# Cache pages on GpSimd's queue, a later sum of log f, later first pages and gathered conv outputs in a recurrent-and-attention decoder step

## Chip, cores and metric

One core of one Trainium2 chip (trn2). The metric is the device time of one execution of the program in microseconds, of which the median over several runs is given. Below, PE is TensorE, DVE is VectorE, ACT is ScalarE, POOL is GpSimd and SP is SyncE, whose instruction stream is used here only to issue DMAs.

## What is computed

One layer of a decoder trunk on 512 prompt positions and 8 sample positions (520 columns), all with the same weights, in float32 with D = 1024. Cut to what matters:

```
h = RMSNorm(x) * (1 + scale1) + shift1                 # adaLN: scale, shift, gate from c @ ada_w
z = h @ w_in -> xr | gr | q | k | v | forget logits | gA | gB
branch A: xc = causal width-4 conv(xr); RG-LRU scan(xc); * gelu(gr); @ w_proj_a
          conv_new = last 3 inputs of the conv, per prompt and sample      (an output)
branch B: logf = log_sigmoid(fl + b_f)
          prompt: softmax(q k / 8 + sum of logf from key to query) v
          sample: the same, with 1024 past rows of each sample taken from pages of a cache
                  (8 samples x 8 pages of 128 rows; a page table says which)
x += gate1 * ((sigmoid(gA) * A @ w_proj_a + sigmoid(gB) * B @ w_proj_b) @ w_o)
x += gate2 * SwiGLU(RMSNorm(x) ...); final RMSNorm
```

The forget logits of prompt and samples give log f, which is an output too, and whose running sum over the prompt positions enters the scores.

## The kernel before

Everything lies transposed, features on the partitions and the 520 positions along the columns, in two halves of 260. A weight matrix is cut into units of 1024 x 128. SP loads two units at a time into a buffer `wraw` (there are two), ACT rounds a unit into a high part `whi`, DVE subtracts for the low part `wlo`, and PE makes each product of 128 output features from three matmuls (high x high, low x high, high x low) for each of the 8 slices of 128 rows and each half, 48 matmuls in all. `product` does this; its first step, `begin`, counts the product (`state["n"]`), calls `tick`, and then loads and splits weights ahead.

The order of the program's text is: q0 to q5 (by a code of their own), q6, q7 (products 0 and 1), then the recurrent stage in pairs of feature tiles (i = 0, 2, 4, 6): `conv(i)`, gates and gelu of the pair before, `conv(i + 1)`, `gate_a`, `lru_gates`, `gate_b`, `lru_exp`. These are products 2 (xr0) to 31 (gr7). Product 32 is k0, and then come the products with w_proj_a (pa0 to pa7) and v0, then attention, merge, w_o and the feed-forward part. The scheduler of the language may move an instruction within its engine, mostly close to its place in the text; each engine then runs its list in that order and waits where an operand or a buffer is not there.

Work on the cache is spread over the products by `tick`. `KEYS[n]` says how many key pages (or half-width pairs of pages, for the first two samples, while only one half of q is there) product n loads; `VALUES` are the products at which a page of values may be used. A page goes into one of seven buffers `pgp`, which the adaLN weights `araw` also use, by `page_load`: SP reads the page's number from the page table into a register (L617) and issues the load (L618); every fourth load back must have been issued first. `key_sums` does the dot products of loaded pages on DVE, a multiplication by the broadcast q (`qb`) and a reduction per head (L662, L663 for half-width pairs, L667, L668 for pages), `state["age"]` ticks after their load: 1 up to q7, 2 from xr0 on. For four pages (`POOL_KEYS`) the multiplication is POOL's (L649). `past_turn` and `past_sums` make the suffix sums of the past log f that `past_softmax` adds to the sums; `past_sums` is PE work (L398, L399).

`forget_logits` and `log_forget` make log f of the new positions. The logits go through DRAM to be spread over 128 partitions; a chain of some 20 small DVE instructions makes log f; it is stored as an output and to `lfd` in DRAM (L586, L587), read back with heads on partitions (L588), summed along the prompt by a DVE scan into `fcs` (L590), and that is stored (L591) for the attention stage.

`conv(i)` evacuates the product twice on ACT (L884, L885), adds the three delayed inputs on DVE (L893, L894), and has three POOL copies put the new conv state into `conv_out` (L895 to L897), which SP stores at the end of the stage (L1027).

Of the kernel before, what the change touches and what calls it, by code (L numbers as in the profile page):

```python
# [8 lines left out]
F32 = mybir.dt.float32  # L9
# [3 lines left out]
ALU = mybir.AluOpType  # L13
# [5 lines left out]
NP = 512  # L19
# [5 lines left out]
KT = 8  # L25
# [39 lines left out]
def kernel(ctx, tc, xT, par, gates, b_f, cst, cse, own, cache_k, cache_v, cache_lf, pt,  # L65
# [103 lines left out]
    def flush():  # L169
        while stores:  # L170
# [1 line left out]

    later = {}

    KEYS = dict(zip(range(42), (2, 0, 0, 2, 3, 2, 3, 2, 0, 1, 1, 1, 2, 2, 2, 1, 0, 1, 0, 1, 2, 2, 2, 2, 0, 1, 1, 1, 2, 2, 1, 2,
                                1, 1, 1, 1, 1, 1, 1, 1, 0, 0)))
# [400 lines left out]
    def log_forget():  # L577
        a = small("fa", 128, LC, 1)
        e = small("fe", 128, LC, 1)
        l1 = small("fl1", 128, LC, 1)  # L580
        sp.dma_start(a, flat(fld))
        act.activation(e, a, AF.Abs)
        act.activation(e, e, AF.Exp, scale=-1.0)
        log1p("fz", e, LC, l1)
        dve.scalar_tensor_tensor(a, a, 0.0, l1, ALU.min, ALU.subtract)
        sp.dma_start(flat(lfT), a)  # L586
        sp.dma_start(flat(lfd), a)  # L587
        sp.dma_start(lf, lfd)  # L588
        fcs = slot("fcs", NP, parts=H)
        dve.tensor_tensor_scan(fcs, one_col[:H].to_broadcast([H, NP]), lf[:, :NP], 0.0, ALU.mult, ALU.add)  # L590
        sp.dma_start(ftd, fcs)  # L591
# [15 lines left out]


    S = []
    loads = []  # L610

    def page_load(cache, s, j, pg=None, c0=0, c1=D):
        if pg is None:
            pg = pgp.tile([128, D], F32, name="pg", tag="pg")
        n = s * NPAGE + j
        with tc.issue_after(loads[-4].ins) if len(loads) >= 4 else nullcontext():
            r = sp.value_load(ptb[0:1, n:n + 1], min_val=0, max_val=NPOOL - 1)  # L617
        loads.append(sp.dma_start(pg, cache[bass.ds(r, 1), :, c0:c1].rearrange("a p c -> (a p) c")))  # L618
        return pg

    qb = {}
# [17 lines left out]
    def key_page(s, j, half=None):  # L639
        if half is not None:  # L640
            return key_halves(s, j, half)
        if j == 0:
            t = pgp.tile([128, D], F32, name="qb", tag="pg")
            sp.dma_start(t, qtd[s:s + 1, :].partition_broadcast(128))
            qb[0] = t
        pg = page_load(cache_k, s, j)
        late = s * NPAGE + j in POOL_KEYS
        if late:
            pool.tensor_tensor(pg, pg, qb[0], ALU.mult)  # L649
        pend.append([0, s, j, pg, None if late else qb[0], None])  # L650

    def key_sums():
        for p in pend:
            p[0] += 1
        while pend and pend[0][0] >= state["age"]:
            _, s, j, pg, q, half = pend.pop(0)
            r = s // 2
            c = 256 * (r % 2) + 32 * j + H * (s % 2)
            with tc.issue_after(state["last"].ins):
                if half is not None:  # L660
                    b, c = 8 * (r % 2) + j, H * (s % 2) + 8 * half
                    dve.tensor_tensor(pg, pg, q.unsqueeze(1).to_broadcast([128, 2, 512]), ALU.mult)  # L662
                    dve.tensor_reduce(S[r // 2].rearrange("p (b c) -> p b c", c=32)[:, b:b + 2, c:c + 8],  # L663
                                      pg.rearrange("p j (h d) -> p j h d", d=DH), AX.X, ALU.add)
                else:
                    if q is not None:
                        dve.tensor_tensor(pg, pg, q, ALU.mult)  # L667
                    dve.tensor_reduce(S[r // 2][:, c:c + H], pg.rearrange("p (h d) -> p h d", d=DH), AX.X, ALU.add)  # L668
# [159 lines left out]
    for i in range(KT):  # L828
# [45 lines left out]
    conv_out = keep.tile([128, KT, 27], F32, name="conv_out")  # L874
    rg_out = keep.tile([128, KT, 9], F32, name="rg_out")
    g = [None] * KT
    lru = {}

    def conv(i):
        xr, xc = slot("xr"), slot("xc")  # L880

        def evac(j, b):
            t0, t1 = HALVES[j]
            act.copy(xr[:, t0:t1], b)  # L884
            act.activation(xc[:, t0:t1], b, AF.Identity, scale=cw[3], bias=prm[:, i, P_CB:P_CB + 1])  # L885

        cw = [prm[:, i, P_CW + n:P_CW + n + 1] for n in range(4)]
        sc = prm[:, i, P_SC:P_SC + 24].rearrange("p (s n) -> p n s", n=3)
        co = conv_out[:, i, 3:27].rearrange("p (s n) -> p n s", n=3)
        product(f"xr{i}", h, evac)  # L890
        for n in range(3):
            d = 3 - n
            dve.scalar_tensor_tensor(xc[:, d:NP], xr[:, :NP - d], cw[n], xc[:, d:NP], ALU.mult, ALU.add)  # L893
# [65 lines left out]
    def both(fn, i):  # L959
        fn(i)  # L960
        fn(i + 1)
# [19 lines left out]
    state["age"] = 2  # L981
    for i in range(0, KT, 2):
        conv(i)
        if i == 0:
            q_done(*q_last)
            past_sums(0)
            ada_piece(1, 6)
            ada_load(1, 7)
        else:
            both(lru_root, i - 2)  # L990
            gelu(i - 2)
            lru_scan(i - 2)
        conv(i + 1)
        if i == 0:
            past_sums(1)
            ada_piece(1, 7)
            ada_copy(1)
        else:
# [4 lines left out]
        if i < 6:  # L1003
# [4 lines left out]
            gate_a(i + 1)  # L1008
            lru_gates(i + 1)
            gate_b(i)  # L1010
            gate_b(i + 1)
            both(lru_exp, i)
            if i == 2:
                log_forget()
        else:
            lru_gates(i)
            gate_a(i)
# [6 lines left out]
            both(lru_scan, i)  # L1024
            both(lru_mul, i)
            both(lru_g, i)
    sp.dma_start(convT, conv_out)  # L1027
    sp.dma_start(rgT, rg_out)

# [548 lines left out]
```

## Time and profile before

| | us |
|---|---|
| runs | 1097.44, 1098.28, 1098.85 |
| median | 1098.28 |
| the profiled execution | 1096.58 |
| its span, from first to last instruction | 1094.8 |
| PE busy | 1038.4 (95%) |
| DVE busy | 667.5 (61%) |
| ACT busy | 499.8 (46%) |
| POOL busy | 165.5 (15%) |

All views below are of the profiled execution, times in us from its first instruction. The chain that ended last is followed back from the last instruction, at each step to what released it; 71% of the span on it are PE's and 12% DVE's. In lists of waits the numbers are the total, how many times, and the longest. In rows of a stage stand its length and then the busy time of each engine with the number of its instructions, the clock granted to PE, the busy share of the DMA engines and GB/s. A row of the order of work has the start, the time taken, the engine (SPq is SP's sequencer), the source line and the operands, and in brackets how long the engine stood idle before it and what ended that. "L210" is a line of the kernel before.

### The profile page before, as it was taken

Reading aid. Unit: us, or ns where it says so; the run is one execution under the profiler, and the core shown is the slowest. Engines: PE = TensorE matmul, PEld = TensorE weight load, DVE = VectorE, ACT = ScalarE, POOL = GpSimd, SP = SyncE. Lnnn points to the kernel's source line nnn. Section 1 sums busy time; section 2 is a strip of 40 time slices with the busy share of each in tenths; the row PEclk is TensorE's granted clock in tenths of the full one; section 3 lists DMA queues with packets and bytes.
Section 4 is the critical chain, followed back from the end, with each engine's and each line's share of the span. In section 5 each row is a group of like instructions: output and inputs, shape, how many; then the busy total and the mean of one; then the engine's idle time right before and its main releaser. Section 6 shows DMA issues by size and latency. Waiting matters only on the chain.

```text
span 1094.8 us, 21019 instructions
## 1 busy us (share of the span) xinstructions
PE 1038.4 (95%) x8210; PEld 955.2 (87%) x8210; DVE 667.5 (61%) x1158; ACT 499.8 (46%) x972; POOL 165.5 (15%) x269
## 2 busy tenths in 40 slices
PE   4998999979999999989999999999999999999996
PEld 2876799969888987778888889999999999999995
DVE  5438699978979876667665544943343333433354
ACT  4513466746683256557787323542222223222352
POOL 1212100000403034325330001500000000000013
PEclk8999999999999999889999999999999999999998
DMA  9797985859777988889775683222232332323212
GB/s 331 261 305 268 325 299 161 267 161 304 243 231 250 320 263 260 248 249 255 231 235 175 232 298 108 79 78 78 90 104 78 103 90 78 116 78 95 79 59 79
DMA packets 167333, 206.95 MB, mean 189 GB/s; under 512 B 9778, under 2 KB 126018, under 8 KB 167170
## 3 DMA queue, kind: packets, MB, share of 16 engines
q1 hardware_dynamic: 163154, 197.62, 57.2%
q10 hardware_dynamic: 3680, 6.42, 1.6%
q0 software_dynamic: 400, 1.57, 0.5%
q8 instruction: 64, 1.05, 0.4%
q14 instruction: 35, 0.29, 0.1%
HBM read 192.49 MB, written 13.09 MB: 188 GB/s over the span
## 4 chain that ended last, share of the span: by engine, by line
PE 71%; DVE 12%; DMA 6%; ACT 5%; issue 3%; SPq 1%; POOL 1%; POOLq 0%; ACTq 0%; DVEq 0%
PE fig L245 11%; PE fiu L245 10%; PE fo L245 10%; PE pa L245 4%; PE pb L245 4%; PE v L245 3%; PE gb L245 3%; PE xr L245 3%; PE k L245 3%; PE wo L245 3%; PE pv L750 2%; DMA araw<-in_ada_w_dram 2%; PE qp L467 2%; DVE wlo L211 2%; DVE pg L667 2%
## 5 line engine op out<-in xcount | busy, mean ns | idle before, releaser
L211 DVE TENSOR_TENSOR wlo<-wraw,whi 128x1024 fp32r<-128x1024 f32 (+1 forms) x131 | 160.4, 1225 | 152.0 <-ACT whi L210 147.2
L210 ACT CAST whi<-wraw 128x1024 fp32r<-128x1024 f32 (+1 forms) x131 | 136.8, 1044 | 234.9 <-PE fo L245 74.5
L245 PE MATMUL fiu<-h2h,wlo 128*128 128x260 f32 x320 | 90.6, 283 | 0.0
L245 PE MATMUL fig<-h2h,wlo 128*128 128x260 f32 x320 | 90.5, 283 | 0.0
L245 PE MATMUL fig<-h2h,whi 128*128 128x260 f32 x320 | 90.3, 282 | 0.0
L245 PE MATMUL fiu<-h2h,whi 128*128 128x260 f32 x320 | 90.3, 282 | 0.0
L245 PE MATMUL fig<-h2l,whi 128*128 128x260 f32 x320 | 90.1, 282 | 0.0
L245 PE MATMUL fiu<-h2l,whi 128*128 128x260 f32 x320 | 90.1, 281 | 0.0
L245 PE MATMUL fo<-ach,wlo 128*128 128x260 f32 x292 | 82.6, 283 | 0.0
L245 PE MATMUL fo<-ach,whi 128*128 128x260 f32 x292 | 82.5, 283 | 0.0
L245 PE MATMUL fo<-acl,whi 128*128 128x260 f32 x292 | 82.4, 282 | 0.0
L337 POOL TENSOR_TENSOR ss<-ss,sq 128x260 f32<-128x260 f32 x18 | 13.6, 756 | 419.8 <-ACT sq L336 419.4
L245 PEld LDWEIGHTS fiu<-h2l,whi 128*128 128x128 f32 x320 | 60.5, 189 | 0.0
L245 PEld LDWEIGHTS fig<-h2l,whi 128*128 128x128 f32 x320 | 60.5, 189 | 0.0
L245 PEld LDWEIGHTS fiu<-h2h,whi 128*128 128x128 f32 x320 | 60.2, 188 | 0.0
L245 PEld LDWEIGHTS fig<-h2h,whi 128*128 128x128 f32 x320 | 60.2, 188 | 0.0
L245 PEld LDWEIGHTS fig<-h2h,wlo 128*128 128x128 f32 x320 | 60.2, 188 | 0.0
L245 PEld LDWEIGHTS fiu<-h2h,wlo 128*128 128x128 f32 x320 | 60.1, 188 | 0.0
L667 DVE TENSOR_TENSOR pg<-pg,qb 128x1024 f32<-128x1024 f32 x44 | 55.5, 1274 | 5.1 <-DMA pg<-in_cache_k_dram 5.0
L668 DVE TENSOR_REDUCE S<-pg 128x16 f32<-128x1024 f32 x48 | 57.5, 1207 | 0.2
L245 PEld LDWEIGHTS fo<-ach,whi 128*128 128x128 f32 x292 | 55.0, 188 | 0.0
L245 PEld LDWEIGHTS fo<-acl,whi 128*128 128x128 f32 x292 | 54.9, 188 | 0.0
(386 smaller groups left out, 3429.8 us busy)
## 6 DMA issues: line engine op xcount, KB each, us to landing
pg<-in_cache_v_dram SPq DMA_DIRECT2D x64, 512.0 KB, 4.6
araw<-in_ada_w_dram SPq DMA_DIRECT2D x48, 512.0 KB, 7.6
pg<-in_cache_k_dram SPq DMA_DIRECT2D x48, 512.0 KB, 4.6
wraw<-in_w_fi_dram SPq DMA_DIRECT2D x44, 512.0 KB, 5.1
wraw<-in_w_in_dram SPq DMA_DIRECT2D x34, 512.0 KB, 7.3
wraw<-in_w_in_dram SPq DMA_DIRECT2D x11, 1024.0 KB, 6.1
pg<-in_cache_k_dram SPq DMA_DIRECT2D x32, 256.0 KB, 4.5
wraw<-in_w_fo_dram SPq DMA_DIRECT2D x8, 1024.0 KB, 5.2
```

Of the source, the lines that this page charges most:

```text
L210: state["act"] = act.copy(hi[:, :k1 - k0], src)
L211: state["last"] = dve.tensor_tensor(lo[:, :k1 - k0], src, hi[:, :k1 - k0].bitcast(F32), ALU.subtract)
L245: state["mm"] = pe.matmul(out[:, :HALF], lhsT=wt[k], rhs=at, start=k == 0 and m == 0, stop=k == nk - 1 and m == 2)
L337: eng.tensor_tensor(acc[:, t0:t1], acc[:, t0:t1], q_, ALU.add)
L467: state["mm"] = pe.matmul(b[:, :HALF], lhsT=wt, rhs=at[:, t0:t1], start=k == 0 and m == 0, stop=k == 3 and m == 2)
L667: dve.tensor_tensor(pg, pg, q, ALU.mult)
L668: dve.tensor_reduce(S[r // 2][:, c:c + H], pg.rearrange("p (h d) -> p h d", d=DH), AX.X, ALU.add)
L750: pe.matmul(pv[0][32 * gq:32 * gq + 32, :], lhsT=pw[r][:, c:c + 32], rhs=pgs[gq // 2][:, 512 * hf:512 * hf + 512], start=j == 0, stop=j == ...
```

## The change

- `page_load` and the full-width q broadcast go through POOL's DMA queue up to product 31 (`LAST_LRU = 32`, as the count is raised before `tick`), and through SP's after that. Each queue keeps its own list of loads.
- The ticks after q3 and q4 are gone; the first pages are loaded after q5. `KEYS` gives 2, 2, 2, 0, 3, 3, 3, 2, 1 at products 0 to 8 instead of 2, 0, 0, 2, 3, 2, 3, 2, 0. The age of a sum is 1 up to product 3 and 2 from product 4 on.
- `POOL_KEYS` is gone: all pages are multiplied on DVE. DVE clears the end of `pw` instead of POOL.
- `log_forget` (at the end of pair 2) ends with the store to `lfd`; the read back, the scan and its store are `sum_forget`, called at the end of pair 4.
- The sample part of the last q tile (`q_done`) moves from behind xr0 to between its two halves. `past_sums` moves from behind xr0 and xr1 to behind gb0 and gb1.
- `conv` copies the last 11 columns of its input with one ACT copy into `conv_tail`; four POOL copies at the end of the stage put together `conv_out`, which now has one of the 60 `heap` slots.

```
-    KEYS = dict(zip(range(42), (2, 0, 0, 2, 3, 2, 3, 2, 0, 1, 1, 1, 2, ...
+    KEYS = dict(zip(range(42), (2, 2, 2, 0, 3, 3, 3, 2, 1, 1, 1, 1, 2, ...
-    POOL_KEYS = (41, 44, 47, 50)
+    LAST_LRU = 32
...
         sp.dma_start(flat(lfd), a)
+    def sum_forget():
         sp.dma_start(lf, lfd)
         fcs = slot("fcs", NP, parts=H)
         dve.tensor_tensor_scan(fcs, one_col[:H].to_broadcast([H, NP]), lf[:, :NP], 0.0, ALU.mult, ALU.add)
         sp.dma_start(ftd, fcs)
...
+        eng = pool if state["n"] <= LAST_LRU else sp
+        done = loads[eng]
+        with tc.issue_after(done[-4].ins) if len(done) >= 4 else nullcontext():
+            r = eng.value_load(ptb[0:1, n:n + 1], min_val=0, max_val=NPOOL - 1)
+        done.append(eng.dma_start(pg, cache[bass.ds(r, 1), :, c0:c1].rearrange("a p c -> (a p) c")))
...
-            sp.dma_start(t, qtd[s:s + 1, :].partition_broadcast(128))
+            (pool if state["n"] <= LAST_LRU else sp).dma_start(t, qtd[s:s + 1, :].partition_broadcast(128))
...
-        late = s * NPAGE + j in POOL_KEYS
-        if late:
-            pool.tensor_tensor(pg, pg, qb[0], ALU.mult)
...
     def tick(keys, values):
+        state["age"] = 1 if state["n"] < 5 else 2
...
-        pool.memset(t[:, 256:], 0.0)
+        dve.memset(t[:, 256:], 0.0)
...
-        if i in (3, 4, 5):
+        if i == 5:
             tick(2, 0)
...
-        pool.tensor_copy(conv_out[:, i, 0:3], xr[:, NP - 3:NP])
-        pool.tensor_copy(co[:, 0:2], sc[:, 1:3])
-        pool.tensor_copy(co[:, 2], xr[:, NP:])
+        act.copy(conv_tail[:, i], xr[:, NP - 3:])
...
-        conv(i)
+        conv(i, None if i else lambda: q_done(*q_last))
         if i == 0:
-            q_done(*q_last)
-            past_sums(0)
...
             gate_b(i)
+            if i == 0:
+                past_sums(0)
             gate_b(i + 1)
+            if i == 0:
+                past_sums(1)
             both(lru_exp, i)
             if i == 2:
                 log_forget()
+            if i == 4:
+                sum_forget()
...
+    for n in range(2):
+        pool.tensor_copy(co[:, :, :, n], sc[:, :, :, n + 1])
+    pool.tensor_copy(co[:, :, :, 2], conv_tail[:, :, 3:])
+    pool.tensor_copy(conv_out[:, :, 0:3], conv_tail[:, :, 0:3])
     sp.dma_start(convT, conv_out)
```

More of the change, by code (lines that the diff above doesn't have):

```diff
@@ L173 @@
     later = {}
-    KEYS = dict(zip(range(42), (2, 0, 0, 2, 3, 2, 3, 2, 0, 1, 1, 1, 2, 2, 2, 1, 0, 1, 0, 1, 2, 2, 2, 2, 0, 1, 1, 1, 2, 2, 1, 2,
+    KEYS = dict(zip(range(42), (2, 2, 2, 0, 3, 3, 3, 2, 1, 1, 1, 1, 2, 2, 2, 1, 0, 1, 0, 1, 2, 2, 2, 2, 0, 1, 1, 1, 2, 2, 1, 2,
                                 1, 1, 1, 1, 1, 1, 1, 1, 0, 0)))
     VALUES = (19, 21, 23, 25, 27, 29, 31, 35, 37, 39)
-    POOL_KEYS = (41, 44, 47, 50)
+    LAST_LRU = 32
     def load_chunks(upto):
@@ L609 @@
     S = []
-    loads = []
+    loads = {pool: [], sp: []}
     def page_load(cache, s, j, pg=None, c0=0, c1=D):
@@ L643, in key_page @@
             t = pgp.tile([128, D], F32, name="qb", tag="pg")
-            sp.dma_start(t, qtd[s:s + 1, :].partition_broadcast(128))
+            (pool if state["n"] <= LAST_LRU else sp).dma_start(t, qtd[s:s + 1, :].partition_broadcast(128))
             qb[0] = t
         pg = page_load(cache_k, s, j)
-        late = s * NPAGE + j in POOL_KEYS
-        if late:
-            pool.tensor_tensor(pg, pg, qb[0], ALU.mult)
-        pend.append([0, s, j, pg, None if late else qb[0], None])
+        pend.append([0, s, j, pg, qb[0], None])
     def key_sums():
@@ L665, in key_sums @@
                 else:
-                    if q is not None:
-                        dve.tensor_tensor(pg, pg, q, ALU.mult)
+                    dve.tensor_tensor(pg, pg, q, ALU.mult)
                     dve.tensor_reduce(S[r // 2][:, c:c + H], pg.rearrange("p (h d) -> p h d", d=DH), AX.X, ALU.add)
@@ L877, with conv @@
     lru = {}
-    def conv(i):
+    def conv(i, mid=None):
         xr, xc = slot("xr"), slot("xc")
@@ L887, in conv @@
         cw = [prm[:, i, P_CW + n:P_CW + n + 1] for n in range(4)]
-        sc = prm[:, i, P_SC:P_SC + 24].rearrange("p (s n) -> p n s", n=3)
-        co = conv_out[:, i, 3:27].rearrange("p (s n) -> p n s", n=3)
-        product(f"xr{i}", h, evac)
+        product(f"xr{i}", h, evac, mid)
         for n in range(3):
@@ L994 @@
         if i == 0:
-            past_sums(1)
             ada_piece(1, 7)
@@ L1026 @@
             both(lru_g, i)
+    co = conv_out[:, :, 3:27].rearrange("p k (s n) -> p k s n", n=3)
+    sc = prm[:, :, P_SC:P_SC + 24].rearrange("p k (s n) -> p k s n", n=3)
+    for n in range(2):
+        pool.tensor_copy(co[:, :, :, n], sc[:, :, :, n + 1])
+    pool.tensor_copy(co[:, :, :, 2], conv_tail[:, :, 3:])
+    pool.tensor_copy(conv_out[:, :, 0:3], conv_tail[:, :, 0:3])
     sp.dma_start(convT, conv_out)
```

7 lines of the change are left out of this document (2 added, 5 removed).

## The prediction

> **What bounds the kernel now.** I read the page first, then for whom TensorE (PE) waits between 60 and 335 us, then the busy time of the engines by stage, and then the order of work on VectorE (DVE) and ScalarE (ACT) around each stall. The page's list of the chain that ended last begins with feed-forward matmuls (fig, fiu, fo), which the change leaves alone. What it edits lies ahead of 335 us, so it can win only the waits there.
>
> ```profile
> span 1094.8 us, 21019 instructions
> ```
> ```profile
> PE ada L308 <- DMA araw<-in_ada_w_dram: 6.4, 2, 4.0
> PE ga L245 <- ACT tA L974: 3.3, 1, 3.3
> PE gate L916 <- ACT gate L917: 2.5, 1, 2.5
> PE pa L245 <- DVE gl L279: 2.3, 1, 2.3
> ```
> ```profile
> 117.00:137.00 20.00, 20.00 (x152) 16.56 (x151) 16.57 (x37) 10.78 (x20) 1.36 (x4) 1.00 0.93 304
> 137.00:226.00 89.00, 88.23 (x730) 86.55 (x728) 88.71 (x122) 59.80 (x99) 3.62 (x5) 1.00 0.75 240
> 226.00:252.00 26.00, 20.86 (x150) 19.05 (x151) 17.82 (x25) 14.44 (x30) 0.77 (x5) 0.93 0.60 182
> ```
>
> The stage rows give PE, weight loads, DVE, ACT and GpSimd (POOL) in this order. From 137 to 226 us DVE works 88.71 of 89 us: it is full, and falls behind PE. From 226 to 252 us PE then stands, and DVE too. The work of the two engines there says why.
>
> ```profile
> 225.68 0.17 DVE L942 TENSOR_TENSOR gate<-gate,th 128x8 f32<-128x8 f32 x1
> 232.32 1.21 DVE L590 TENSOR_TENSOR_SCAN fcs<-one_col,lf 16x512 f32<-16x512 f32 x1 [6.46 <-DMA lf<-lfd]
> 233.46 0.71 DVE L893 SCALAR_TENSOR_TENSOR xc<-xr,prm,xc 128x509 f32<-128x509 f32 x1
> ```
> ```profile
> 225.88 0.20 ACT L952 COPY rg_out<-gate 128x9 f32<-128x9 f32 x1 [3.66 <-DVE gate L942]
> ...
> 226.98 0.59 ACT L885 ACTIVATE xc<-xr,prm 128x260 f32<-128x260 f32 x1
> ...
> 235.83 0.63 ACT L278 CAST xch<-xc 128x520 fp32r<-128x520 f32 x1 [6.29 <-DVE xc L893]
> ```
> ```profile
> 225.06 2.13 DMA lfd<-fa
> 227.21 5.09 DMA lf<-lfd
> ```
>
> DVE stands 6.46 us for log f, which makes a round trip through DRAM: written in 2.13 us, read back in 5.09. Behind the scan in DVE's order stands the convolution, ACT's split (xch) waits 6.29 us for that, and the 3.3 us of ga on ACT follow.
>
> SyncE's queue (SP) is the other suspect.
>
> ```profile
> SPq L186 <- DVE wlo L211: 360.7, 43, 18.5
> ...
> SPq L618 <- DVE S L668: 36.5, 20, 4.6
> ```
>
> Weight loads (L186) wait 360.7 us for a buffer that DVE's split frees, pages (L618) for a buffer that DVE's sums free. DVE holds both, not SP. So I put nothing down for the move of the pages by itself: no PE wait above is one for weights.
>
> **The change, term by term.** *Sum of log f a pair later.* Gone from its old place are the idle 6.46 and the scan. The convolution then starts when ACT has evacuated its input, at 226.98 + 0.59 = 227.57 instead of 233.46: **-5.9**. What is late next is ACT's read of DVE's last scan (225.88), which stays. At the new place the load of log f still is issued there and takes up to 5.09; the long part of the round trip, the DVE chain and the write, lies behind by then, and SP may run ahead. Between 0 and +5.1 I take **+1.0**, nearer to 0, since load and scan are traced together and the load has no other producer left. The scan itself is worth 233.46 - 232.32 = 1.14 wherever it stands: **+0.5** between 0 (in one of DVE's waits for ACT) and 1.1. SP's store of the result (ftd) now waits there for the scan; behind it are weight loads that wait for DVE anyway.
>
> *First pages later.* The first loads come two q tiles later. By the tick counts 10 sums are done before gb0 now and 8 then; from the eleventh product on the totals agree.
>
> ```profile
> L663 DVE TENSOR_REDUCE S<-pg x10: 1173/1218/1221, 81.2 to 132.4; 128x16 f32<-128x1024 f32 x10
> ```
> ```profile
> 128.71 1.22 DVE L662 TENSOR_TENSOR pg<-pg,qb 128x1024 f32<-128x1024 f32 x1
> ...
> 133.49 0.69 DVE L279 TENSOR_TENSOR xcl<-xc,xch 128x520 fp32r<-128x520 f32 x1
> ```
>
> Two of them took 133.49 - 128.71 = 4.8 us where DVE had room (16.57 of 20 busy); in the full stretch they cost 4.8. Against that, the suffix sums leave the two conv products for gb0 and gb1:
>
> ```profile
> 115.88 0.86 PE suf L398 x2
> ...
> 125.41 0.86 PE suf L399 x2
> ```
>
> These are the first and last of four such pieces, 4 x 0.86 = 3.4 us of PE. PE gets to ga0 so much earlier, and DVE's full stretch starts earlier with it. Net **+1.4** (from -3.4, if DVE finds other room for the pages, to +4.8, if it starts no earlier).
>
> *Pages multiplied on DVE, not POOL.* Four products leave POOL.
>
> ```profile
> 280.83 6.05 POOL L649 TENSOR_TENSOR pg<-pg,qb 128x1024 f32<-128x1024 f32 x1 [6.50 <-DMA pg<-in_cache_v_dram]
> ```
> ```profile
> 284.59 2.31 DVE L942 TENSOR_TENSOR gate<-gate,th 128x8 f32<-128x8 f32 x1
> ...
> 295.78 2.30 DVE L942 TENSOR_TENSOR gate<-gate,th 128x8 f32<-128x8 f32 x1
> ```
> ```profile
> 318.67 4.56 DVE L667 TENSOR_TENSOR pg<-pg,qb 128x1024 f32<-128x1024 f32 x2
> ...
> 332.49 1.78 DVE L279 TENSOR_TENSOR gl<-ge,gh 128x520 fp32r<-128x520 f32 x1
> ```
> ```profile
> 136.93 2.35 DVE L662 TENSOR_TENSOR pg<-pg,qb 128x1024 f32<-128x1024 f32 x2
> ```
>
> While POOL multiplied, an 8-column DVE instruction took 2.31 and 2.30 instead of 0.17, a pair of products 4.56 instead of 2.35, and gl 1.78 instead of 0.69: 2.14 + 2.13 + 2.21 + 1.09 = 7.6 us of DVE lost. The four products cost DVE 4 x (2.35 - 1.22) = 4.5. DVE sets the chain there (ACT's gate and pa's gl above wait for it): **-3.1**, from -7.6 (the products find gaps) to +4.5 (the lost time hid behind ACT's waits). The Trainium skill, "SBUF — State Buffer", section "Who interferes with whom", states the same: a DVE instruction with two SBUF inputs and a GpSimd instruction that reads SBUF lock each other out. The trace agrees with its 2.31 us.
>
> *Pages through POOL's queue.* A POOL issue of a 256 KB row block and its landing are known from four broadcasts.
>
> ```profile
> qb<-qtd POOLq DMA_DIRECT2D x4, 256.0 KB, 6.4
> ```
> ```profile
> pg<-in_cache_k_dram SPq DMA_DIRECT2D x32, 256.0 KB, 4.5
> ```
> ```profile
> L635 POOL DMA_DIRECT2D qb<-qtd x4: 545/553/593, 72.7 to 125.3; - x4
> ```
>
> The issue costs POOL 0.55 us, and POOL is nearly idle (3.62 of 89 us). Landing takes 6.4 us against 4.5 for a page of the same size on SP: 1.9 more. A sum comes two products after its load, so most pages don't show that. The tightest one in the full stretch does:
>
> ```profile
> 215.52 0.34 SPq L618 DMA_DIRECT2D pg<-in_cache_k_dram  x1
> ```
> ```profile
> 220.05 1.22 DVE L667 TENSOR_TENSOR pg<-pg,qb 128x1024 f32<-128x1024 f32 x1
> ```
>
> It is used 4.5 us after its issue and would come 1.9 late. A page that stands behind a weight load on SP today would go out earlier on POOL: between -0.5 and +1.9 I take **+0.9**. What stands behind a waiting page on POOL is the suffix adds (needed only after gb0 now) and the q copies. No weights stand behind it any more.
>
> *The adaLN weights.* The longest PE wait, 4.0 us, is for araw in the first conv product:
>
> ```profile
> 92.02 10.23 SPq L186 DMA_DIRECT2D wraw<-in_w_in_dram  x2
> ```
> ```profile
> 103.47 6.02 DMA araw<-in_ada_w_dram
> ```
>
> SP gets rid of the pages ahead of the first of these weight loads, but the second waits for the past log f pages to be turned on PE, after q7, and araw stands behind it. That order stays. Pages from POOL may now share those 6.02 us: from -4.0 (wait gone) to +3.0 (half as many bytes again in the same stretch), I take **+0.5**.
>
> *Conv outputs.* Eight ACT copies at the 0.20 us of the rg_out copy above make 1.6 us on an engine with 29 of 89 us free: **+0.4**, between 0 and 1.6. The 24 small POOL copies of now hid in POOL's idle time, so their removal gives 0. The four gathers at the end stand behind POOL's last pages, and convT's store holds SP meanwhile:
>
> ```profile
> 326.65 0.39 SPq L186 DMA_DIRECT2D wraw<-in_w_pa_dram  x1
> ```
> ```profile
> 353.31 5.95 PE pa L245 x48
> ```
>
> The load behind it, now at 326.65, feeds the fourth pa product at 353.31. A store that held SP for ten us more would not show: 0, and if that cover went, what exceeds it. The clearing of pw moves to DVE (three times ahead of 335, by the 0.17 us of the small DVE instruction above): **+0.5**, between 0 and that. q7's transposes in the middle of xr0 are the same PE work: 0.
>
> **Sum.** -5.9 + 1.0 + 0.5 + 1.4 - 3.1 + 0.9 + 0.5 + 0.4 + 0.5 = **-3.8 us**. The profiled execution took 1096.58 us (its span 1094.8 and 1.8 around it), 1.7 less than the runs' median of 1098.28. Against the former that makes 1092.8, against the median, which I forecast, **1094.5 us**.
>
> **Rivals.** *The wait only moves.* If the load of log f goes out when DVE already stands at the scan, 5.1 comes back instead of 1.0: 1094.5 + 4.1 = 1098.6, no change. For it: SP waits hundreds of us for DVE and so seldom runs far ahead. Against it: the old wait also held the write.
>
> *The first stage opens.* The clock granted to PE (third number from the end) sags with that wait:
>
> ```profile
> 100.00:117.00 17.00, 12.99 (x75) 9.05 (x75) 11.15 (x29) 6.97 (x15) 9.35 (x18) 0.90 0.85 300
> ```
>
> With SP free of pages the araw may go out ahead of the blocked weight load; the 4.0 us go, and of the 17 us at 0.90 some 1.5 come back: 1094.5 - 0.5 - 5.5 = 1088.5. Against it: nothing in the change touches the order of those two.
>
> *POOL's queue starves DVE (the other side).* Place: the full stretch.
>
> ```profile
> L618 SPq DMA_DIRECT2D pg<-in_cache_k_dram x18: 333/343/512, 137.5 to 225.7; - x18
> ```
>
> Eighteen key pages are issued there in 89 us, each as soon as DVE frees a buffer. If landing is 1.9 us longer for all and n of them have no slack, DVE, which takes its work in order, loses 1.9 n. With four it is 7.6, the gain is gone and the time 1094.5 - 0.9 + 7.6 = 1101.2; from three on (1099.3) it is above today's. For it: the 220.05 page. Against it: no DVE wait for a page is recorded in that stretch, which leaves 0.3 us idle in all.
> The Trainium skill, same page, section "SBUF: two separate sides", goes further: a DMA from GpSimd's queue waits for its descriptors while DVE runs in a two-port mode, 620 ns becoming about 3100. By that, an estimate, each page would be 2.5 us later still. DVE's work here is two-input arithmetic and sums, and the 545 to 593 ns of POOL's four issues show no such wait; no run here shows what 80 issues in a full stretch do.
>
> **How the numbers follow.** A time within 0.2%, 2.2 us, can't be told from no change. The forecast case, 1089.5 to 1096.5, has 0.47, the opened first stage 0.10, the wait that only moves (1096 to 1100) 0.20, the starved DVE (1099 to 1107) 0.18, and 0.05 is left for something else that is slower. Faster: 0.47 x 0.95 + 0.10 + 0.20 x 0.3 = 0.61. Same: 0.02 + 0.20 x 0.6 + 0.18 x 0.2 = 0.18. Slower: the rest, 0.21. The range for 8 in 10, 1086.5 to 1102, leaves out the upper part of the starved case and the far end of the opened one; the likeliest case's own is 1089.5 to 1096.5.
>
> **What would show it.** Right: no DVE wait for log f at the place of the old one; PE's wait in ga gone; the 8-column DVE instruction at 0.2 us throughout; DVE full from about 134 us; POOL's issues near 0.6 us. Wrong: DVE waits for pages between 137 and 300 us (the starved case), a DVE wait of some 5 us for log f near 270 us (the wait moved), the araw wait shorter or longer than 4 us, or SP held long at convT with pa waiting for weights. The prediction falls most easily with the 1.4: if the full stretch doesn't start earlier, PE's stall after 226 us comes back by 3.4.

## The result, and the profile after

The changed kernel took 1081.03 us (median of four runs, 1080.17 to 1082.19) beside 1097.86 for the kernel before in the same session: a ratio of 0.9849, 95% interval 0.9832 to 0.9866, or 16.6 us. The forecast was a gain of 3.8 us, and the time lies below the range's lower end of 1086.5. The profiled execution took 1082.19 us.

First PE's waits between 60 and 335 us of the changed kernel (total, times, longest).

```profile
span 1080.5 us, 21007 instructions
```
```profile
PE ada L308 <- DMA araw<-in_ada_w_dram: 4.8, 2, 4.4
PE qt L796 <- ACT q L271: 1.5, 1, 1.5
PE ga L245 <- DVE pw L721: 1.1, 1, 1.1
PE pa L245 <- DVE gl L279: 0.8, 1, 0.8
PE gate L914 <- ACT tA L972: 0.6, 1, 0.6
```

Of the four long waits of before, those of ga for ACT (3.3) and of gate (2.5) are gone, and pa's for gl is down from 2.3 to 0.8. The wait for araw is still there, 4.4 us, in another place. Now the busy time by stage, of the kernel after and, for two stages not shown yet, of the one before (PE, weight loads, DVE, ACT, POOL with their instructions, granted clock, DMA share, GB/s).

```profile
60.00:75.00 15.00, 15.00 (x123) 11.49 (x123) 6.57 (x13) 4.32 (x10) 2.38 (x7) 1.00 1.01 306
100.00:117.00 17.00, 12.03 (x85) 9.12 (x85) 13.28 (x27) 5.84 (x13) 11.00 (x23) 0.91 1.00 357
137.00:226.00 89.00, 87.34 (x698) 83.53 (x697) 88.97 (x115) 57.89 (x104) 12.66 (x24) 1.00 0.74 234
226.00:252.00 26.00, 26.00 (x215) 23.97 (x214) 22.68 (x27) 12.52 (x24) 5.28 (x10) 1.00 0.76 233
300.00:340.00 40.00, 39.22 (x318) 36.58 (x317) 37.19 (x53) 20.97 (x33) 14.77 (x19) 1.00 0.82 272
```
```profile
60.00:75.00 15.00, 12.59 (x85) 7.48 (x84) 5.39 (x11) 2.56 (x5) 1.65 (x5) 0.91 0.97 298
...
300.00:340.00 40.00, 35.00 (x268) 32.51 (x269) 34.36 (x41) 28.75 (x51) 5.50 (x4) 0.96 0.74 241
```

The matmul counts tell more than the busy times. From 226 to 252 us PE did 150 matmuls before and does 215 now, from 300 to 340 us 268 and 318. At 26.00 / 215 = 0.121 us each that is 7.9 and 6.1 us of work that is done earlier.

For where each microsecond comes from, here is the start of the first of a product's matmuls in the traces (each product is 48 matmuls, and they are counted so): the kernel before, and the difference to it of the changed kernel and of five experiments described below.

| start of | before | changed | changed, pages on SP | queue alone | later pages alone | log f alone | multiplies alone |
|---|---|---|---|---|---|---|---|
| xr1 | 118.53 | -13.9 | -16.2 | -6.4 | -15.5 | -0.3 | -0.6 |
| ga1 | 134.84 | -7.2 | -12.8 | -6.4 | -12.1 | -0.3 | -0.6 |
| gb2 | 191.96 | -1.5 | -8.3 | -3.9 | -7.3 | -0.3 | -0.6 |
| gb4 | 252.24 | -10.2 | -17.0 | -12.6 | -6.1 | -9.0 | -0.6 |
| gr6 | 310.63 | -13.8 | -20.7 | -12.7 | -6.2 | -7.5 | -3.2 |
| pa1 | 339.76 | -17.7 | -24.6 | -12.0 | -5.8 | -7.4 | -7.1 |
| the 1009th fo matmul | 1076.59 | -17.4 | -25.3 | -11.1 | -4.8 | -7.5 | -7.7 |
| end of the span | 1094.8 | -14.3 | -26.2 | -8.1 | -5.7 | -8.4 | -8.6 |

The changed kernel wins 7.2 us up to ga1, gives 5.7 back in DVE's full stretch (the suffix sums, 3.4, are paid there), wins 8.7 at the old log f wait and 3.6 and 3.9 at the two later stalls, and loses 3.1 between the 1009th fo matmul and the end.

### The profile page after: what moved, and what is told of

Read it like the earlier page. It is cut to its first block, busy times and chain, and to the rows that moved or that the text cites. A ratio compares the mean times of both kernels' runs of the same rounds, so it can differ in the third digit from the quotient of the medians.

```text
span 1080.5 us, 21007 instructions
## 1 busy us (share of the span) xinstructions
PE 1029.1 (95%) x8210; PEld 951.7 (88%) x8210; DVE 663.9 (61%) x1166; ACT 494.4 (46%) x976; POOL 192.2 (18%) x328
## 4 chain that ended last, share of the span: by engine, by line
PE 74%; DVE 10%; DMA 7%; ACT 4%; issue 3%; POOL 1%; SPq 0%; POOLq 0%; DVEq 0%; ACTq 0%
PE fig L245 11%; PE fiu L245 11%; PE fo L245 10%; PE v L245 4%; PE pb L245 4%; PE pa L245 4%; PE k L245 4%; PE gb L245 3%; DMA wraw<-in_w_in_dram 3%; PE pv L751 3%; PE wo L245 3%; PE xr L245 2%; PE gr L245 2%; DMA araw<-in_ada_w_dram 2%; PE qp L467 2%
## 5 line engine op out<-in xcount | busy, mean ns | idle before, releaser
L667 DVE TENSOR_TENSOR pg<-pg,qb 128x1024 f32<-128x1024 f32 x48 | 58.1, 1222 | 4.4 <-DMA pg<-in_cache_k_dram 4.3
L622 POOL DMA_DIRECT2D pg<-in_cache_k_dram x66 | 35.2, 533 | 111.4 <-DVE S L668 59.8
```

What stands on the lines that cost most here:

```text
L622: done.append(eng.dma_start(pg, cache[bass.ds(r, 1), :, c0:c1].rearrange("a p c -> (a p) c")))
```

## The experiments

Ratios are to the kernel before, run on the same chip, with 95% intervals; times are medians of several runs. One per cent is 11 us.

| run | us | ratio | interval |
|---|---|---|---|
| changed, pages on SP | 1070.33 | 0.9758 | 0.9721 to 0.9795 |
| queue alone | 1086.40 | 0.9921 | 0.9894 to 0.9947 |
| changed, POOL's queue in the first stage only | 1076.74 | 0.9805 | 0.9781 to 0.9830 |
| changed, POOL's queue after the first stage only | 1073.99 | 0.9796 | 0.9768 to 0.9824 |
| log f later alone | 1088.08 | 0.9912 | 0.9879 to 0.9944 |
| changed, log f early | 1084.83 | 0.9884 | 0.9845 to 0.9922 |
| changed, pages on SP, log f early | 1080.79 | 0.9845 | 0.9821 to 0.9868 |
| multiplies on DVE alone | 1088.68 | 0.9938 | 0.9912 to 0.9964 |
| changed, four multiplies on POOL | 1087.38 | 0.9910 | 0.9882 to 0.9938 |
| first pages later alone | 1092.55 | 0.9960 | 0.9939 to 0.9982 |
| changed, first pages early | 1079.54 | 0.9854 | 0.9810 to 0.9898 |
| first pages later and log f later | 1081.63 | 0.9851 | 0.9801 to 0.9900 |
| suffix sums later alone | 1098.64 | 1.0030 | 1.0008 to 1.0052 |
| changed, pages on SP, suffix sums old | 1072.25 | 0.9770 | 0.9741 to 0.9800 |
| changed, pages on SP, conv outputs old | 1072.86 | 0.9775 | 0.9730 to 0.9821 |
| changed, pw cleared on POOL | 1082.52 | 0.9860 | 0.9821 to 0.9900 |
| changed, pages on SP, pw cleared on POOL | 1072.06 | 0.9772 | 0.9745 to 0.9800 |
| pages later, log f later, multiplies on DVE | 1072.48 | 0.9776 | 0.9749 to 0.9803 |

### The queue

Pages back on SP, nothing else undone in the source:

```diff
-    LAST_LRU = 32
+    LAST_LRU = -1
```

> The changed kernel with one part undone: all pages and q broadcasts go through SP's queue again (LAST_LRU = -1). Theory A (each stall that went belongs to the part of the change that names it; the queue as such is worth nothing, as predicted): 1080 to 1083 us, the first stage starts ga0 as early as in the changed kernel (within 1 us). Theory B (the queue is what opened the first stage: with pages on SP the adaLN weights and the log f load wait behind page buffers): 1087 to 1092 us, PE waits again for araw in or near xr0 with 8 us lost by ga0, and the log f chain on DVE falls back from about 125 us to about 200 us. Starved-DVE theory (POOL's queue costs 1.9 us per page in the full stretch, hidden under the other gains): faster than the changed kernel, 1074 to 1079 us.

1070.33 us: the queue costs the changed kernel 10 us (0.9758 beside 0.9849). Theory B has the wrong sign, A's 0 failed too, and of the starved case only the sign held, with a larger size and, as the next runs show, another place. The table has it: 5.6 us by ga1, 1.2 more by gb2, 1.0 between pa1 and the 1009th fo matmul, and at the end the lead of the version with pages on SP grows from 7.9 to 11.9. On the kernel before, the queue alone:

```diff
-        loads.append(sp.dma_start(pg, ...))
+        eng = pool if state["n"] <= LAST_LRU else sp
+        done.append(eng.dma_start(pg, ...))
```

> The kernel before with one part alone: pages and q broadcasts up to the recurrent branch's end through POOL's queue. The prediction's term (+0.9): 1098 us. Theory Q (the queue costs what its undoing gave, 11 us, of which about 4 us are a longer drain of POOL at the end of the program and the rest waits for pages): 1104 to 1109 us. Theory H (in the kernel before, whose early pages stand in SP's queue between the adaLN weights, it frees SP: first stage 4 to 8 us shorter, end 4 us longer): 1092 to 1098 us. In each case but the first POOL's drain behind its last multiply takes about 9.5 us instead of 2.5.

There it wins 8.7 us (1 - 0.9921 of 1097), more than any of the three texts allowed. In its trace it wins in two places, 6.4 us up to ga1 and 8.7 between gb2 and gb4, though the sum of log f stands at its old place, and gives back 2.5 between these and 3.0 at the end. Here are SP's rows of log f in the kernel before and then, of the run with the queue alone, SP's and the last of DVE's (start, time taken).

```profile
181.07 0.34 SPq L581 DMA_DIRECT2D fa<-fld  x1
```
```profile
108.31 0.66 SPq L582 DMA_DIRECT2D fa<-fld  x1
...
132.25 1.35 SPq L588 DMA_DIRECT2D lfd<-fa  x1
137.87 0.33 SPq L589 DMA_DIRECT2D lf<-lfd  x1
```
```profile
206.00 1.20 DVE L591 TENSOR_TENSOR_SCAN fcs<-one_col,lf 16x512 f32<-16x512 f32 x1
```

With no pages ahead in SP's queue the logits are fetched at 108 instead of 181 us, log f is read back 68 us before the scan, and nobody waits. So the queue removes, by another road, stalls that the later pages and the later sum remove too. Beside these only its price is left. Two runs split it by place:

```diff
-        eng = pool if state["n"] <= LAST_LRU else sp
+        eng = pool if state["n"] in ON_POOL else sp      # range(0, 7); and range(7, 33)
```

> The changed kernel with POOL's queue for the pages of the first stage alone (up to the tick of ga1), SP's queue for all later ones: 33 transfers are issued from POOL instead of 92. TensorE's order is that of the changed kernel. Theory Q1 (the queue costs by place: 5.6 us in the first stage, where POOL's pages take the DMA engines from the adaLN weights, some 1.3 later, and 4 at the end, by a drain that grows with the number of transfers issued from POOL): 1075 to 1078 us, ga1 starts as in the changed kernel (127.6 us) with an araw wait of some 4 us, and the drain takes 2.48 + 28 x 0.081 = 4.75 us, which the last stores hide. Theory Q2 (each page from POOL lands later and DVE pays for it throughout): 1077 to 1080 us, ga1 1 to 2 us earlier. Theory Q3 (the drain does not depend on the number): it still takes 9.5 us, 1079 to 1081 us.

> The complement: SP's queue for the pages of the first stage, POOL's for those after ga1 (63 transfers issued from POOL). Theory Q1: the first stage is that of the changed kernel with all pages on SP (ga1 near 122 us, no araw wait over 1 us), the drain takes 2.48 + 58 x 0.081 = 7.2 us, of which some 1.6 to 2 show: 1072 to 1075 us. Theory Q2: 1075 to 1079 us, lost bit by bit between 130 and 420 us. Q3: a drain of 9.5 us, 1074 to 1076 us.

Both fell where theory Q1 put them. With POOL's queue in the first stage only, ga1 starts at 126.61 us and the araw wait is 4.6 us; with the complement ga1 starts at 121.66 and no araw wait is over 0.7.

Why the queue costs 5.6 us in the first stage is open, though. Theory Q1 has it that POOL's pages take the DMA engines from the adaLN weights, but PE's own order differs too: the scheduler put the last adaLN piece (`ada`) before ga0 in both runs that have POOL's queue in the first stage beside the later pages, and behind the gates of ga0 in both that have SP's. PE's rows in the changed kernel and then with all pages on SP:

```profile
115.06 1.92 PE L308 MATMUL ada<-araw,silc 128*32 128x512 f32 x4 [4.42 <-DMA araw<-in_ada_w_dram]
117.35 1.92 PE L308 MATMUL ada<-araw,silc 128*32 128x512 f32 x4 [0.36 <-DMA araw<-in_ada_w_dram]
119.20 0.58 PE L245 MATMUL ga<-hh,whi 128*128 128x260 f32 x1
```
```profile
117.59 0.28 PE L914 MATMUL gate<-xcl,gws 128*128 128x260 f32 x1
118.57 1.05 PE L308 MATMUL ada<-araw,silc 128*32 128x512 f32 x4 [0.70 <-DMA araw<-in_ada_w_dram]
...
122.07 0.37 PE L245 MATMUL ga<-hh,whi 128*128 128x260 f32 x1
```

The weights that end the wait come earlier in the changed kernel (115.06) than with pages on SP (118.57); with pages on SP PE has done ga0 by then. No two runs that differ in the queue alone have the same order, so what the transfers cost and what the order costs was not separated.

These are the rows of POOL's drain at the end of the program: before, changed, first stage only, after the first stage only (the third figure, the longest, is the one that counts, in ns).

```profile
L1562 POOLq DRAIN  x3: 40/107/2480, 1087.5 to 1094.5; - x3
```
```profile
L1568 POOLq DRAIN  x3: 46/104/9531, 1070.2 to 1080.2; - x3
```
```profile
L1568 POOLq DRAIN  x3: 46/104/4682, 1072.3 to 1078.2; - x3
```
```profile
L1568 POOLq DRAIN  x3: 50/104/7243, 1062.9 to 1070.7; - x3
```

With 5, 92, 33 and 64 transfers issued from POOL (the text had counted 63) it took 2.48, 9.53, 4.68 and 7.24 us: about 0.081 us for each, as worked out beforehand from the first two (4.75 and 7.2). It runs while the last stores land; from the 1009th fo matmul to the end it is 21.3 us in the changed kernel and 17.3 with all pages on SP, so 4.0 us of it show.

### The sum of log f

```diff
             if i == 2:
                 log_forget()
-            if i == 4:
                 sum_forget()
```

> The changed kernel with one part undone: the sum of log f stands again directly behind its chain, at the second pair (i == 2). Theory A (the wait for the round trip through DRAM was worth all that PE gained between 222 and 252 us, 8.7): 1087 to 1090 us, with a DVE wait of about 6 us for log f near 215 us. The prediction's term (-5.9 + 1.0 + 0.5 = -4.4 undone): 1085.4 us. Theory B (the queue moved off SP lets the load of log f and its chain run early, so that the wait is gone wherever the sum stands): 1081 to 1083 us, no DVE wait for log f over 1 us.

> The changed kernel with two parts undone: pages on SP's queue and the sum of log f directly behind its chain (i == 2). Beside the one with pages on SP alone (1070.3 us). Theory L (the wait of DVE for the round trip costs PE only where DVE is already behind; with an open first stage DVE has some 10 us in hand): 1069 to 1072 us, with a DVE wait for log f of 5 to 7 us in the trace and no PE stall behind it. The prediction's term (-4.4 undone): 1074.7 us, a PE wait in ga4 or ga5.

> The kernel before with one part alone: the sum of log f a pair later. The prediction's terms (-5.9 + 1.0 + 0.5): 4.4 us faster than the kernel before, ratio 0.996. Theory R (what it is worth is the PE stall between 222 and 252 us; with pages on SP the later sum was worth 10.5 us beside the run that undid it): 8 to 11 us faster, ratio 0.990 to 0.993, PE's waits in gate and ga at 229 to 252 us gone. Theory P (DVE has so much work left at that place that it is late anyway, and later stalls take back the gain): 1 to 4 us faster.

The third, the move alone on the kernel before, gave 9.6 us (1 - 0.9912 of 1097), as theory R had it. In its trace 8.7 lie between gb2 and gb4. The stage from 226 to 252 us of that run:

```profile
226.00:252.00 26.00, 26.00 (x215) 23.97 (x215) 24.81 (x30) 12.57 (x24) 0.12 (x1) 1.00 0.88 277
```

With pages on SP, undoing it cost 9.5 us (0.9845 beside 0.9758). Theory L, which said nothing would show, failed, and the prediction's 4.4 is under half of it: DVE waited 7.6 us for log f and PE stood. With pages on POOL the undoing cost 3.8 (0.9884, with an interval that just reaches the changed kernel's 0.9849), and none of it there. The scan and the stage of that run:

```profile
220.49 1.21 DVE L592 TENSOR_TENSOR_SCAN fcs<-one_col,lf 16x512 f32<-16x512 f32 x1 [4.75 <-DMA lf<-lfd]
```
```profile
226.00:252.00 26.00, 26.00 (x215) 23.97 (x214) 25.93 (x33) 15.60 (x32) 3.70 (x7) 1.00 0.78 246
```

DVE waits 4.75 us, but the wait ends 12 us earlier than in the kernel before, while PE is where it was (gr3 begins at 222.55 us, before at 222.06), and PE does its 215 matmuls. Beside the changed kernel that run's trace starts gr3 1.9 us later, and the rest is lost behind 400 us. Why the move back touches these was not settled.

### The multiplies

```diff
+        late = s * NPAGE + j in POOL_KEYS
+        if late:
+            pool.tensor_tensor(pg, pg, qb[0], ALU.mult)
```

> The changed kernel with one part undone: four of the late pages (numbers 41, 44, 47, 50) are multiplied by q on POOL again. Theory A (the two PE stalls between 298 and 335 us, 3.6 and 3.8, hung on these four): 1087 to 1089 us, 8-column DVE instructions of 2.3 us and a gl of 1.8 us are back, and PE waits for the gate and for gl. The prediction's term (-3.1 undone): 1084.1 us. Rival D (those stalls went because DVE arrives earlier after the log f wait went; the multiplies are worth only the DVE time at them): 1081 to 1083 us.

> The kernel before with one part alone: no page is multiplied on POOL. The prediction's term: 3.1 us faster, ratio 0.997. Theory A (as its undoing from the changed kernel, 6.3): 6 to 7 us faster, ratio 0.994, the wait of pa for gl down from 2.3 to under 1 us and the 8-column DVE instructions at 0.2 us. Theory P (DVE is late there for other reasons): within 2 us.

Undone, 6.7 us (0.9910 beside 0.9849); alone, 6.8: theory A both times. Rows of DVE with the multiplies on POOL again, then in the changed kernel, then the stage from 300 to 340 us of the run with the move alone, and last the same work of PE, from gb4 to pa1, before and with the move alone.

```profile
304.43 4.54 DVE L672 TENSOR_TENSOR pg<-pg,qb 128x1024 f32<-128x1024 f32 x2
...
318.24 2.06 DVE L280 TENSOR_TENSOR gl<-ge,gh 128x520 fp32r<-128x520 f32 x1
```
```profile
304.78 2.35 DVE L667 TENSOR_TENSOR pg<-pg,qb 128x1024 f32<-128x1024 f32 x2
...
316.52 0.69 DVE L279 TENSOR_TENSOR gl<-ge,gh 128x520 fp32r<-128x520 f32 x1
```
```profile
300.00:340.00 40.00, 39.25 (x320) 36.20 (x320) 35.19 (x46) 26.68 (x44) 4.59 (x6) 1.00 0.78 244
```
```profile
252.24:339.76 87.52, 82.36 (x648) 75.47 (x647) 78.48 (x91) 58.81 (x100) 17.55 (x10) 0.98 0.78 255
```
```profile
251.60:332.67 81.07, 80.32 (x649) 73.93 (x647) 72.45 (x91) 58.73 (x100) 3.32 (x5) 1.00 0.85 267
```

A pair of products takes 4.54 us instead of 2.35 and gl 2.06 instead of 0.69 while POOL multiplies. Without that PE does 320 matmuls in the 40 us instead of 268. From gb4 to pa1 DVE's own time even falls, from 78.48 to 72.45 us: it does 14 page products there instead of 12, and the other two of the four stand behind pa1.

### First pages and suffix sums

```diff
-        if i == 5:
+        if i in (3, 4, 5):
             tick(2, 0)            # and the old KEYS and ages
```

> The changed kernel with one part undone: the first pages are loaded from the fourth q tile on again (old ticks, old numbers, old ages), all else as changed. Theory G (the first pages crowd the first stage, whatever queue they take: they share seven buffers and the DMA engines with the adaLN weights): 1090 to 1095 us, araw waits of 4 us and more around xr0, and ga1 starts 6 us or more later. Theory H (the crowding is in SP's queue alone, and POOL's queue cures it too): 1079 to 1083 us. The prediction's term for the first pages (4.8 us of DVE work that returns to a stage with room): 1076 us.

> The kernel before with one part alone: the first pages from the sixth q tile on. The prediction's term for this part alone (+4.8 us, since the suffix sums stay where they were): 1102 us. Theory G (the first pages crowd the first stage): 1082 to 1090 us, ga1 starts 6 to 12 us earlier and the 4.0 us wait for araw in xr0 is gone. Theory H (only together with the other parts): 1095 to 1099 us.

> The kernel before with two parts: first pages from the sixth q tile on, and the sum of log f a pair later; pages on SP. Theory R (the later pages open the first stage by 12 us, and what they lose again in the full stretch and at the log f wait comes from that wait): 13 to 16 us faster, ratio 0.985 to 0.988. Sum of the single terms as predicted for the sum of log f and as measured for the pages (-4.4 - 4.1): 8.5 us faster, 0.992. If the two overlap as the queue and the pages do: no more than the better of the two alone.

Alone on the kernel before, the later pages start ga1 12.1 us earlier, with pages still on SP: theory G's sign. The time, 1092.55 us, lies in the range of no text. The only wait of PE listed between 60 and 137 us is the first row; below it stand the two later stages.

```profile
PE adat L320 <- ACT adas L313: 0.8, 1, 0.8
```
```profile
137.00:226.00 89.00, 83.81 (x683) 81.35 (x683) 82.13 (x115) 55.55 (x94) 7.55 (x7) 1.00 0.79 249
226.00:252.00 26.00, 21.18 (x150) 18.46 (x148) 23.39 (x31) 13.14 (x27) 0.44 (x3) 0.87 0.49 153
```

About half is lost again: 4.8 us between ga1 and gb2, in the full stretch, and 1.2 by gb4, with DVE's wait for log f at 7.5 us in this run; 4.4 are left by the ratio. Together with the later sum it is 16.3 us (interval 11.0 to 21.8). In that run's trace each takes its own place, 7.5 us by gb2 and 8.8 more by gb4, so these two do not overlap; whether they win more than their sum, 4.4 + 9.6, as theory R had it, the interval leaves open. In the changed kernel the undoing shows nothing (0.9854 beside 0.9849): there the queue has already opened the stage (theory H).

The suffix sums and q7's transposes at their new place, alone on the kernel before, and moved back in the version with pages on SP:

```diff
-        if i == 0:
-            q_done(*q_last)
-            past_sums(0)          # past_sums(1) after xr1 likewise: now behind gb0 and gb1
```

> The kernel before with one part alone: the suffix sums stand at the two gb products and the transposes of q7 in the middle of xr0. The prediction's term (-3.4, since PE gets to ga0 earlier and DVE's full stretch starts earlier): 1093.5 us. Rival (PE's suffix sums only filled a time in which PE waited for araw, and the full stretch takes back what is won): 1096 to 1098 us.

> The changed kernel with two parts undone: pages on SP's queue, and the suffix sums and q7's transposes back in the two first conv products. Beside the one with pages on SP alone (1070.3 us). Prediction's term (PE reaches ga0 3.4 us earlier by the move): undone 1072 to 1074 us. Rival R1 (3.4 us of PE work are moved and nothing else: PE is the bound there, the loss at xr1 comes back at gb1): 1069.5 to 1071 us. Rival R2 (the move by itself loses, as it did on the kernel before, 3 us): 1067 to 1069 us.

Alone the move loses 3.3 us (interval 0.9 to 5.7), and neither of the two texts for it fits; beside the others it is worth 1.3, with intervals of 3 to 4 us to each side, too wide to tell the three texts apart.

### The small parts, and all that counts together

> The changed kernel with two parts undone: pages on SP's queue, and the conv outputs copied on POOL tile by tile again. Beside the one with pages on SP alone (1070.3 us). Prediction's term (eight ACT copies, +0.4): 1069.9 us, no difference. Rival (24 small POOL copies that read SBUF lengthen DVE's instructions beside them in the full stretch): 1072 to 1075 us, with conv or page instructions on DVE above their usual 0.7 and 1.2 us.

> The changed kernel with one small part undone: the clearing of 24 columns of pw stands on POOL again. In the changed kernel PE waits 1.1 us in ga3 for this clearing on DVE and loses 2.3 us between gb2 and gr3. Theory E (the clearing on DVE in program order is what costs it): 1079 to 1080 us, the wait gone. Theory F (DVE is full there, so PE would wait for the next thing that DVE is late with): 1081.0 us, no difference. Prediction's term (+0.5 undone): 1080.5 us.

> The changed kernel with two parts undone: pages on SP's queue, and the clearing of 24 columns of pw on POOL. Beside the one with pages on SP alone (1070.3 us). Theory E (0.7 us of PE's wait in ga3 goes, and the slower clock behind it): 1069 to 1070 us. Theory F (PE waits for the next thing DVE is late with, as in the run with POOL's queue, where this was worth nothing): 1070 to 1072 us.

Conv outputs back to 24 POOL copies, and pw cleared on POOL (`pool.memset` for `dve.memset`): none differs measurably from the run that it is set beside. For the conv outputs the time alone, 1072.86 us, would also suit the rival (1072 to 1075), but its sign is missing: between 117 and 340 us of that trace a single DVE instruction, at 327.8 us, took more than 0.06 us over its usual time. In the changed kernel with pw cleared on POOL the 1.1 us of PE are still there, for the next DVE instruction in the line (theory F):

```profile
PE ga L245 <- DVE S L719: 1.2, 1, 1.2
```

Last, three parts on the kernel before, with pages on SP, suffix sums and conv outputs left alone:

> The kernel before with three parts: first pages from the sixth q tile on, the sum of log f a pair later, no page multiplied on POOL; pages stay on SP, suffix sums and conv outputs stay where they were. Theory T (these three carry the gain, and each takes away a stall of its own): 15.0 for the first two together and 6 to 8 for the third make 1073 to 1076 us, ratio 0.978 to 0.981. If they carry all of it: 1070 us, 0.976. If the third overlaps with the others, as pages later and the queue do: 1079 to 1082 us.

0.9776 (0.9749 to 0.9803), beside 0.9758 for the version with pages on SP: within their intervals these three carry all of it. This version, or the changed kernel with pages on SP, beats both kernels, the latter the changed one by 10 us.

## Why the prediction was wrong

It had the sign and a right reading of two stalls, that for log f and that beside POOL's multiplies. The sizes were wrong nearly everywhere, and for the first pages and the queue so was the mechanism.

| term | forecast | alone on the kernel before | in the changed kernel |
|---|---|---|---|
| log f a pair later | -5.9 + 1.0 + 0.5 = -4.4 | -9.6 | -3.8; -9.5 with pages on SP |
| first pages later | +4.8 | -4.4 | 0 |
| suffix sums later | -3.4 | +3.3 | not run; with pages on SP -1.3, within the intervals |
| multiplies on DVE | -3.1 | -6.8 | -6.7 |
| queue, with the adaLN weights | +0.9 + 0.5 | -8.7 | +10 |
| conv outputs, pw | +0.4 + 0.5 | not run | 0 (conv with pages on SP) |

*Log f.* "The convolution then starts at 227.57 instead of 233.46: -5.9" was right for DVE and wrong for PE. The row from 226 to 252 us, shown in the prediction, had more in it: 20.86 us busy for 150 matmuls is 0.139 each against 0.121. So 5.1 us were PE standing, and 150 x 0.018 = 2.7 went to matmuls that took longer. Part of the 2.7 is the clock; the row's 0.93 stood there, and I used such a row in a rival only. Two finer rows of the kernel before, the first right behind ga's wait of 3.3 us and the second behind pa's of 2.3:

```profile
246.30:249.60 3.30, 3.26 (x15) 3.26 (x16) 3.30 (x5) 2.02 (x6) 0.00 (x0) 0.50 0.92 319
```
```profile
335.00:338.40 3.40, 3.17 (x14) 3.17 (x15) 3.32 (x7) 0.12 (x1) 0.35 (x1) 0.50 0.96 305
```

At half the clock 15 matmuls took 3.26 us, 0.217 each: some 1.4 us of the 2.7. What the rest is was not traced. The Trainium skill, "TensorE: Matmul & The Clock Gate", Part 1, says that the clock is cut to half after an idle window of about 3.4 us. Here listed waits of 3.3 and 2.3 us were enough, and the clock is 1.00 where the waits are gone. The 1.0 for the new place was 0: no DVE wait for log f is left in the changed kernel, and the rival "the wait only moves" fell with that. The 0.5 for the scan was not measured by itself.

*Multiplies.* The contention of 7.6 us was right. What failed was "the four products cost DVE 4.5" as a cost ahead of pa1: only two more stand there, 2 x 1.22 = 2.4 us, so 5.2 of the 7.6 came back. They did not fill DVE's waits for ACT, as my lower end had it: from gb4 to pa1 these go only from 10.0 to 9.5 us. The clock is part of the 6.8 too: the half clock from 335.0 us, shown above, is gone.

*First pages.* The step that failed is that pages were priced as DVE work alone. The rival "the first stage opens" was set aside with "nothing in the change touches the order of those two"; but the pages' own transfers stood before the araw, and the DMA engines were full (share 0.97 from 60 to 75 us). Four half-width pairs, 2 MB, leave the time up to q5, at 298 GB/s an estimated 7 us of all 16 engines. Whether bytes, SP's order, the seven shared buffers or PE's order, which the scheduler changed with them, count most was not separated; the queue alone, which leaves the bytes, opens 6.4 of the 12.

*Suffix sums.* Moved alone, they let xr1 start 3.4 us earlier, as worked out, but ga1 only 1.6 earlier, and gb2 starts 1.8 later: the 3.4 are paid again behind gb0 and gb1. So "DVE's full stretch starts earlier with it" did not hold there. Why more than that is lost was not traced.

*The queue.* "I put nothing down for the move by itself", since no PE wait was one for weights, missed that log f and the araw stand in SP's queue as well: 8.7 us by itself. The +0.9 for late pages was wrong as well. No DVE wait for a page is recorded between 137 and 335 us, so the rival "POOL's queue starves DVE" did not come in its place, though a loss of its size did: in the first stage, where my adaLN term took +0.5 and allowed at most +3.0 for pages from POOL, and at the end, by the drain, which no term of mine had. Its companion sentence from the Trainium skill, "SBUF — State Buffer", "SBUF: two separate sides", on transfers that wait for DVE, speaks of DVE's two-port modes. Whether DVE ran in one here no run shows, and no such wait shows either: from 130 to 226 us a page takes 4.5 us to land from POOL (median, changed kernel) and 4.8 with pages on SP. This row has POOL's key page issues from 130 to 226 us, where DVE works 88.97 of 89 us:

```profile
L622 POOL DMA_DIRECT2D pg<-in_cache_k_dram x20: 527/527/536, 135.0 to 223.7; - x20
```

*The sum* failed beyond its terms, because the parts are not independent: the first stage is opened by the later pages or by the queue, and the log f wait is hidden by the later sum or by the queue. Whichever of two comes second wins nothing at that place, and its price is still paid.

Signs that came: PE's wait in ga for ACT gone, the 8-column DVE instructions at 0.17, POOL's issues at 0.53 us, no wait for log f. The araw wait "longer or shorter than 4 us" came as 4.4, in ada's last piece. DVE is full from 115 us on in the changed kernel, but for 0.4 us between 125 and 130, earlier than the 134 I gave.

## What to carry to other kernels

Price a stall by the matmuls that its stage does against those of an undisturbed stage, not by the listed waits: that takes the slower clock in. Before a part is given a price, ask which other part of the same change removes the same stall, and which transfer or load (log f here) stands in the queue that is being emptied. Run each part alone and each one undone: a part that wins 8.7 us alone cost 10 beside the rest.

## What the runs showed of the hardware that was not expected

- POOL's drain at the end of a program grows by about 0.081 us for each DMA issued from POOL (2.48, 4.68, 7.24 and 9.53 us for 5, 33, 64 and 92). Up to some 5 us hide behind the last stores.
- At half the granted clock a matmul took 0.217 us instead of 0.121, for 3.4 us, behind listed PE waits of 3.3 and of only 2.3 us.
- The landing of SP's loads of adaLN weights spreads when pages come through POOL's queue, with the DMA engines full (share 1.00 from 100 to 117 us). These two rows have the time from issue to landing of araw between 60 and 125 us (shortest, median, longest) in the changed kernel and with pages on SP. That the longer landing causes the 4.4 us wait is not shown, as PE's order differs between the two.

```profile
DMA to landing us min/median/max: 3.7/9.6/12.9
```
```profile
DMA to landing us min/median/max: 5.8/7.6/9.6
```
